# One decoder layer with top-2 experts on one core: routing of the last tiles in fewer, larger batches, in written order

## The chip, the core and the metric

The kernel is one program on one core of a Trainium2 chip. Five engines work side by side, each through its own list of instructions in order: TensorE (PE in the profile, its weight loads PEld), VectorE (DVE), ScalarE (ACT), GpSimd (POOL) and SyncE (SP), which here issues most transfers. The metric is device time of one execution in microseconds (us); less is better.

## What is computed

A layer of a decoder trunk over 1024 tokens (and 16 meta tokens) of width 1024: a mixer of two head groups, an output projection, a layer normalisation, a mixture of experts, a second normalisation. This case is about the seam between the projection and the experts:

```python
mix = mixed @ w_out                                   # output projection
h = layer_norm(ALPHA * h + mix, ln1_g, ln1_b)
group_prob = softmax(h @ w_group + b_group)           # 4 groups: the best one
in_group = (h @ w_expert + b_expert)[best group]      # its 8 experts: the best two
e_w = softmax(top2(in_group))
for e in range(32):                                   # each token: two of 32 experts
    y += combine[:, e] * (silu(h @ w1[e]) * (h @ w3[e])) @ w2[e]
out = layer_norm(ALPHA * h + y, ln2_g, ln2_b)
```

## The kernel before

Tokens lie in eight tiles of 128. The mixer runs first. Its attention of the last two tiles (6 and 7) ends last, so for tiles 0 to 5 the projection, normalisation and logits are woven into the attention (`p3gen`), and for tiles 6 and 7 they follow it.

For a tile t the steps are: `s0(t)` loads the residual `ht` and transposes and splits the mixed heads into two pieces (`mh`, `ml`, since a float32 product is made of three products of pieces); `s1(t)` makes the product (`omm`, two halves of 512 columns, 12 matrix instructions each), adds it to `ht` on VectorE, takes the statistics (`ln_stats`), applies the normalisation (ScalarE, then gain `g` and shift `b` on VectorE) and stores the tile to `h1d` in memory; `s2(t)` transposes `ht` and makes the 36 router logits `lg`. For tiles 6 and 7 the logits are made from the tile as it is before the normalisation.

Routing of tiles t0 to t1 is two functions. `choose(t0, t1)` is a chain of small VectorE instructions: `first_max` finds the first largest logit (twice for the experts), two-hot rows `oh` and their sum `ohs` follow, then the weights `gate` and the table `rv`. `place(t0, t1)` counts on TensorE how many earlier tokens chose the same expert (into `rq`), reads each token's place `pose`, adds to the running count `cum`, and then, for each tile and choice, compares the place with the slot numbers (`ohp`) and multiplies by `rv`, so that the table `acc` tells which token stands in which slot of which expert. When all eight tiles are in `acc`, `index` makes `ix`, and GpSimd gathers the first expert's 128 rows of `h1d` by it.

The experts then run one after another (`phase4`): 128 gathered rows are transposed and split (`xf`, `xh`, `xl`), multiplied by `w13`, gated (`sg`), multiplied by `w2`, and stored to `ysd`. The weights are loaded by SyncE (`load_raw`) into a ring of buffers, long ahead, and each 512-column piece is split into two on ScalarE and VectorE (`split_k`: `w13h` and `w13l`). Of expert 0's eight pieces six are split; two are used as they are. The last two experts' outputs aren't stored, but added in `finish` by a product with a one-hot matrix; the others come back by gathers with the index `fi`.

The order of the steps around the seam is written as a string, which a loop reads:

```python
SEQ3 = "A1 L4 b04 B1 L4 H5 A9 a46 L3 G3 b46 H6 p0 G9 B9 a67 p1 |0 O2 O1 H7 O9 p2 R3 b68 p5"
for w in SEQ3.split():
    steps[w[0]](*[int(x) for x in w[1:]])
```

A and B advance `s0` of tile 6 and 7 by so many steps, G and O advance `s1` of tile 6 and 7, H is `s2`, L loads so many weight blocks of 1 MB, a is `choose` and b is `place` of a range of tiles, p and R also split pieces of expert 0. What stands before the bar is ordered by the framework's scheduler, what stands behind it keeps the written order on every engine. `p3gen` calls `choose` itself for pairs of tiles up to the tile number `CH_`.

Of the kernel before, what the change touches and what calls it, by code (L numbers as in the profile page):

```python
# [8 lines left out]
F32 = mybir.dt.float32  # L9
F32R = mybir.dt.float32r  # L10
I32 = mybir.dt.int32
AF = mybir.ActivationFunctionType
ALU = mybir.AluOpType
AX = mybir.AxisListType.X
# [3 lines left out]
P = 128  # L18
D = 1024
KT = 8  # L20
SEQ = 1024
NT = 8
# [5 lines left out]
NE = 32  # L28
# [8 lines left out]
TV, TO = (0, 1, 2, 3, 4, 5, 6, 7), (0, 0.75, 1.25, 2.5, 3.25, 4, 4.75)  # L37
TA = (0, 1, 2, 3, 4, 5, 6, 7)
SP0 = 0
PX, CH_ = 6, 4  # L40
H0, HG_, GS = 10, (1, 2), (3, 1)
XB2, MH = 2, 2
RX = 1
SPH = (0, 2, 4, 6, 6, 8, 8)
SEQ3 = "A1 L4 b04 B1 L4 H5 A9 a46 L3 G3 b46 H6 p0 G9 B9 a67 p1 |0 O2 O1 H7 O9 p2 R3 b68 p5"
XN = 3
YB = 2
GE = 5
SPK = ()
# [7 lines left out]
G2 = 3  # L57
# [1 line left out]
MB, BB, WB, TB = 2, 2, 2, 3  # L59
RA, RB, RC = 5, 6, 2  # L60
FE, RL = NE - 8, 4 * (RA + RB + 4 + RC) + 4 + RA
RT = 2
GB = 3 * HA * DH
LN_EPS = 1e-5
RMS_EPS = 1e-6
# [16 lines left out]
class Trunk:  # L82
# [738 lines left out]
    def phase2(self):  # L821
        nc, tc, a, r, small = self.nc, self.tc, self.a, self.rows, self.small
# [255 lines left out]
        O, TQ = {}, ["tp", TB, "tg", TG]  # L1078
# [136 lines left out]
            nc.vector.tensor_scalar(rs[:, 1:2], rs[:, 0:1], -1.0, None, op0=ALU.mult)  # L1215
            nc.vector.scalar_tensor_tensor(lg, lg, rs[:, 1:2], cg[:, 1], op0=ALU.mult, op1=ALU.add)

        def choose(t0, t1, hook=lambda i: None):
            n = t1 - t0
            ts = slice(t0, t1)  # L1220
            rp = O["op"]
# [24 lines left out]
            m = first_max(lg[:, :, :4], 4, oh4)  # L1246
            ex = tl("ex", 4)
            nc.vector.tensor_tensor(ex, lg[:, :, :4], bc(m, 4), op=ALU.subtract)
            hook(0)
            sp, sn = tl("sp", 4), tl("sn", 4)  # L1250
            nc.scalar.activation(sp, ex, AF.Sigmoid)
            nc.scalar.activation(sn, ex, AF.Sigmoid, scale=-1.0)
# [10 lines left out]
            m2 = first_max(ing2, 8, oe[1])  # L1263
            e2 = tl("e2")
            nc.vector.tensor_tensor(e2, m1, m2, op=ALU.subtract)
            hook(1)
            for k in range(2):
                nc.scalar.activation(gate[:, ts, k], e2, AF.Sigmoid, scale=1.0 - 2.0 * k)
            for t in range(n):
# [4 lines left out]
            ohs, rv = O["ohs"], O["rv"]  # L1274
# [12 lines left out]
        def place(t0, t1):  # L1287
            n, ts = t1 - t0, slice(t0, t1)
            ohs, rv = O["ohs"], O["rv"]
# [9 lines left out]
            nc.vector.tensor_reduce(pose[:, ts], px, axis=AX, op=ALU.add)  # L1299
            for t in range(t0, t1):  # L1300
                nc.vector.tensor_tensor(cum, cum, ohs[:, t], op=ALU.add)
            pa = ps.tile([P, 4, P], F32, name="rq", bufs=1)[:, 0, :2 * NE]
            for t in range(t0, t1):
                for k in range(2):
# [100 lines left out]
        def run(gen, n=99):  # L1405
            for _ in range(n):
                next(gen, None)
# [2 lines left out]
        o67 = [s1(6), s1(7)]  # L1410
        self.man, self.pcs0 = ExitStack(), {}

        def split(i):
            self.split_k(self.raws_of(0), range(SPH[i], SPH[i + 1]), self.pcs0, SPK)

        steps = {"L": self.load_raw,
                 "A": lambda n: run(n67[0], n), "B": lambda n: run(n67[1], n),
                 "G": lambda n: run(o67[0], n), "O": lambda n: run(o67[1], n), "H": s2, "p": split,
                 "a": choose, "b": place, "R": lambda n: choose(7, 8, lambda i: split(n + i)),
                 "|": lambda n: self.man.enter_context(tc.manual_schedule())}  # L1420
        for w in SEQ3.split():
            steps[w[0]](*[int(x) for x in w[1:]])
        self.index(acc[:, :NE], NE, self.ix)
        nc.vector.tensor_copy(self.gsl, acc[:, NE:])
        pn = ps.tile([P, 4, P], F32, name=TQ[0], bufs=TQ[1])[:, 0]
        nc.tensor.matmul(pn[:, :NE], ones, cum, start=True, stop=True)
        n1 = small.tile([P, NE], I32, name="n1", bufs=1)
# [49 lines left out]
    def phase4(self):  # L1477
# [127 lines left out]
        self.load_raw(RX)  # L1605
        for e in range(XN):
            gat_(e)
        fi = self.small.tile([P, NT, 2], I32, name="fi", bufs=1)
        eo = mp.tile([P, D], F32, name="y", bufs=YB)
        ev = eo[:, :2 * NT * NE].rearrange("p (t k e) -> p t k e", t=NT, k=2)  # L1610
        fv, fo = [eo[:, D - 2 * NT * (i + 1):D - 2 * NT * i].rearrange("p (t k) -> p t k", k=2) for i in range(2)]
        nc.vector.tensor_tensor(ev, self.oh, self.slots[:, None, None, :NE].to_broadcast([P, NT, 2, NE]), op=ALU.mult)
        nc.vector.tensor_reduce(fv, ev, axis=AX, op=ALU.add)
        nc.vector.scalar_tensor_tensor(fv, fv, float(P), self.pose, op0=ALU.mult, op1=ALU.add)
        nc.vector.tensor_scalar(fo, self.pose, float(P), 4096.0, op0=ALU.is_ge, op1=ALU.mult)
        nc.vector.tensor_tensor(fv, fv, fo, op=ALU.add)
        nc.vector.tensor_scalar(fi, fv, float((NE - 2) * P), None, op0=ALU.min)
        xt = xsplit(xpose(XB[0]))
        gat_(XN)
        self.load_raw(2 + RC - RX)  # L1620
        for e in range(NE):
            more = e + 1 < NE
            ph = up(xt, pcs[e])
            if more:
                self.split_k(self.raws_of(e + 1), range(KT), pcs.setdefault(e + 1, {}))
                tps = xpose(XB[(e + 1) % XN])
                gat_(e + 1 + XN)
                sg = swiglu(ph)
                xt = xsplit(tps)
                if e > 0:  # L1630
                    keep(evac(down(act, pcs.pop(e - 1)), self.gsl[:, e - 1:e]), e - 1)
                act = apose(sg)
                self.split_k(self.raws_of(e), range(KT, 12), pcs[e])
            else:
                self.split_k(self.raws_of(e), range(KT, 12), pcs[e], (), True)
                for i in (1, 0):
                    nc.vector.tensor_tensor(oh[i], self.slots[:, None, :].to_broadcast([P, NT, P]),
                                            ixt[:, i, :, None].to_broadcast([P, NT, P]), op=ALU.is_equal)
                sg = swiglu(ph)
                yo = down(act, pcs.pop(e - 1))  # L1640
                act = apose(sg)
                ys = [[mp.tile([P, D], F32R, name=n, bufs=b) for n, b in (("y", YB), ("xg1", 1))]]
                evac2(yo, self.gsl[:, e - 1:e], ys[0])
# [236 lines left out]
```

## Time and profile before

| | |
|---|---|
| median of 3 runs | 1188.87 us (1187.49 to 1192.16) |
| the profiled execution | 1180.65 us, span 1178.9 us |
| busy share of the span | PE 93%, DVE 73%, ACT 54%, POOL 25% |
| mean granted TensorE clock | 0.957 of full speed |
| mean DMA rate | 230 GB/s |

The span runs from the first to the last instruction of the program; the 1.75 us that the profiled execution takes beyond it lie around the program. A row of the trace gives the start, the duration, the engine, the line, the output and the inputs; a bracket behind it gives how long the engine had been idle and what ended that. Attention ends at about 750 us, the experts run from about 808 to 1124 us, and the last stage from there to the end.

### The profile page before, as it was taken

Reading aid. Unit: us, or ns where it says so; the run is one execution under the profiler, and the core shown is the slowest. Engines: PE = TensorE matmul, PEld = TensorE weight load, DVE = VectorE, ACT = ScalarE, POOL = GpSimd, SP = SyncE. Lnnn points to the kernel's source line nnn. Section 1 sums busy time; section 2 is a strip of 40 time slices with the busy share of each in tenths; the row PEclk is TensorE's granted clock in tenths of the full one; section 3 lists DMA queues with packets and bytes.
Section 4 is the critical chain, followed back from the end, with each engine's and each line's share of the span. In section 5 each row is a group of like instructions: output and inputs, shape, how many; then the busy total and the mean of one; then the engine's idle time right before and its main releaser. Section 6 shows DMA issues by size and latency. Waiting matters only on the chain. (4 is left out here: it accounts for less than half of the span.)

```text
span 1178.9 us, 19811 instructions
## 1 busy us (share of the span) xinstructions
PE 1091.0 (93%) x7061; PEld 932.1 (79%) x7061; DVE 862.4 (73%) x1672; ACT 630.9 (54%) x1310; POOL 289.6 (25%) x389
## 2 busy tenths in 40 slices
PE   6999999999989979899989999866999999999983
PEld 5999999999979968777777777755777777777751
DVE  7941357988532337999848768786999999999946
ACT  3443345755223334556546445234777777777643
POOL 3523102511100013435414322001111111112163
PEclk8999999999989998999989999886999999999997
DMA  7511123457696577886567582576999999599785
GB/s 288 182 59 46 42 93 127 135 166 237 210 241 203 167 246 237 243 231 201 156 199 178 134 297 73 236 281 219 377 398 398 398 406 399 204 366 416 291 213 206
DMA packets 112441, 271.01 MB, mean 230 GB/s; under 512 B 31075, under 2 KB 60523, under 8 KB 99540
## 3 DMA queue, kind: packets, MB, share of 16 engines
q1 hardware_dynamic: 100816, 236.43, 58.4%
q0 software_dynamic: 11232, 32.22, 8.4%
q8 instruction: 57, 0.93, 0.3%
q10 hardware_dynamic: 292, 1.07, 0.2%
q14 instruction: 44, 0.36, 0.1%
HBM read 213.83 MB, written 64.53 MB: 236 GB/s over the span
## 5 line engine op out<-in xcount | busy, mean ns | idle before, releaser
L186 PE MATMUL pj<-hTh,wfh 128*128 128x346 f32 (+1 forms) x480 | 156.3, 326 | 0.0
L187 PE MATMUL pj<-hTl,wfh 128*128 128x346 f32 (+1 forms) x480 | 156.0, 325 | 0.0
L188 PE MATMUL pj<-hTh,wfl 128*128 128x346 f32 (+1 forms) x480 | 155.9, 325 | 0.0
L881 DVE TENSOR_TENSOR_SCAN mm<-mm,zero 128x272 f32<-128x272 f32 (+3 forms) x64 | 89.4, 1410 | 22.0 <-ACT mm L868 19.8
L186 PEld LDWEIGHTS pj<-hTh,wfh 128*128 128x128 f32 x480 | 91.0, 190 | 0.4 <-issue 0.2
L188 PEld LDWEIGHTS pj<-hTh,wfl 128*128 128x128 f32 x480 | 91.0, 190 | 0.1
L187 PEld LDWEIGHTS pj<-hTl,wfh 128*128 128x128 f32 x480 | 90.9, 189 | 0.2
L1535 PE MATMUL ph<-w13h,xh 128*128 128x512 f32 x192 | 88.8, 463 | 0.0
L179 PE MATMUL pj<-wvh,hTl 128*128 128x256 f32 (+3 forms) x280 | 79.7, 287 | 2.6 <-DVE hTl L97 2.6
L178 PE MATMUL pj<-wvl,hTh 128*128 128x256 f32 (+3 forms) x280 | 79.7, 287 | 2.1 <-DVE wvl L97 2.1
L177 PE MATMUL pj<-wvh,hTh 128*128 128x256 f32 (+3 forms) x280 | 80.2, 290 | 0.0
L1465 DVE TENSOR_TENSOR w13l<-raw,w13h 128x512 fp32r<-128x512 f32 x126 | 77.8, 683 | 0.0
L1503 POOL DMA_INDIRECT xg<-h1d,ix x32 | 34.1, 1067 | 171.3 <-PE tp L1513 134.1
L1537 PE MATMUL ph<-w13h,xl 128*128 128x512 f32 x192 | 75.4, 393 | 0.0
L1536 PE MATMUL ph<-w13l,xh 128*128 128x512 f32 x192 | 74.9, 390 | 0.0
L872 POOL TENSOR_SCALAR_AFFINE_SELECT mm<-mm 128x128 f32<-128x128 f32 x64 | 40.2, 634 | 113.5 <-ACT mm L868 113.3
L1464 ACT ACTIVATE w13h<-raw 128x512 fp32r<-128x512 f32 x126 | 68.0, 620 | 0.0
L866 PE MATMUL z<-qk 128*128 128x416 f32 (+6 forms) x224 | 60.7, 378 | 5.8 <-ACT kuw L778 3.8
L868 ACT ACTIVATE mm<-z 128x512 f32<-128x512 f32 (+1 forms) x80 | 44.3, 564 | 40.7 <-PE z L866 31.0
L1465 DVE TENSOR_TENSOR w2l<-raw,w2h 128x512 fp32r<-128x512 f32 x96 | 59.9, 687 | 2.2 <-ACT w2h L1464 0.2
L96 ACT ACTIVATE xh<-tp 128x512 fp32r<-128x512 f32 x64 | 31.5, 492 | 49.9 <-DVE xf L1522 43.1
L902 ACT ACTIVATE wt<-tp 128x512 f32<-128x512 f32 (+1 forms) x80 | 41.6, 556 | 27.2 <-PE tp L901 26.6
(441 smaller groups left out, 2965.8 us busy)
## 6 DMA issues: line engine op xcount, KB each, us to landing
raw<-in_w SPq DMA_DIRECT2D x67, 1024.0 KB, 11.1
ysd<-y POOLq DMA_DIRECT2D x30, 512.0 KB, 8.4
qk<-qkd SPq DMA_DIRECT2D x16, 520.0 KB, 5.8
ht<-hscr SPq DMA_DIRECT2D x16, 512.0 KB, 3.4
wo4h<-in_w SPq DMA_DIRECT2D x8, 1024.0 KB, 12.4
wo4l<-in_w SPq DMA_DIRECT2D x7, 1024.0 KB, 13.3
wo6l<-in_w SPq DMA_DIRECT2D x7, 1024.0 KB, 11.9
wo6h<-in_w SPq DMA_DIRECT2D x7, 1024.0 KB, 10.6
```

The source lines that it names most:

```text
L177: nc.tensor.matmul(o[:p, :n], xh, wh[:, kt, ws], start=(kt == 0), stop=False)
L178: nc.tensor.matmul(o[:p, :n], xh, wl[:, kt, ws], start=False, stop=False)
L179: nc.tensor.matmul(o[:p, :n], xl, wh[:, kt, ws], start=False, stop=(kt == KT - 1))
L186: nc.tensor.matmul(o[:, :n], wh[:, kt], self.hTh[:, kt, c0:c0 + n], start=(kt == 0), stop=False)
L187: nc.tensor.matmul(o[:, :n], wh[:, kt], self.hTl[:, kt, c0:c0 + n], start=False, stop=False)
L188: nc.tensor.matmul(o[:, :n], wl[:, kt], self.hTh[:, kt, c0:c0 + n], start=False, stop=(kt == KT - 1))
L881: nc.vector.tensor_tensor_scan(mm[:, c0:c1][:, ::-1], mm[:, c0:c1][:, ::-1], self.zero1.to_broadcast([P, c1 - c0]), 1.0, op0=ALU.mult, op1 ...
L1464: nc.scalar.activation(wh, raw, AF.Copy)
L1465: (nc.gpsimd if k in pool else nc.vector).tensor_tensor(wl, raw, wh.bitcast(F32), op=ALU.subtract)
L1535: nc.tensor.matmul(ph, xh[:, kt], wh, start=False, stop=False)
L1536: nc.tensor.matmul(ph, xh[:, kt], wl, start=False, stop=False)
L1537: nc.tensor.matmul(ph, xl[:, kt], wh, start=False, stop=(kt == ks[-1]))
```

## The change

- `choose` is called for tiles 0 and 1, 2 to 5, and 6 and 7 (three calls; before: 0 and 1, 2 and 3, 4 and 5, 6, 7). `place` is cut in two: `place` (count, `pose`, `cum`) and `fill` (`ohp`, `acc`), each called for tiles 0 to 5 and then for 6 and 7 (before: 0 to 3, 4 and 5, 6 and 7).
- The bar stands near the front of the string, so that nearly all of the seam keeps the written order.
- All six splits of expert 0 are made in one piece, behind `index`.
- The last three weight blocks of the string are loaded behind the work on tile 7.
- The six instructions that make `fi` move from behind the first gathers to the last expert, ahead of its `w2` splits.

```diff
-PX, CH_ = 6, 4
+PX, CH_ = 6, 2
-SPH = (0, 2, 4, 6, 6, 8, 8)
-SEQ3 = "A1 L4 b04 B1 L4 H5 A9 a46 L3 G3 b46 H6 p0 G9 B9 a67 p1 |0 O2 O1 H7 O9 p2 R3 b68 p5"
+SEQ3 = "A1 B1 L4 L4 |0 H5 A9 B9 a26 G2 x06 O1 G1 y06 O1 H6 O1 G9 H7 O9 L3 a68 x68 y68"
-RT = 2
+RT = 4
-        def choose(t0, t1, hook=lambda i: None):
+        def choose(t0, t1):
...
             for t in range(t0, t1):
                 nc.vector.tensor_tensor(cum, cum, ohs[:, t], op=ALU.add)
+
+        def fill(t0, t1):
+            rv = O["rv"]
             pa = ps.tile([P, 4, P], F32, name="rq", bufs=1)[:, 0, :2 * NE]
             for t in range(t0, t1):
...
-        def split(i):
-            self.split_k(self.raws_of(0), range(SPH[i], SPH[i + 1]), self.pcs0, SPK)
-
-                 "G": lambda n: run(o67[0], n), "O": lambda n: run(o67[1], n), "H": s2, "p": split,
-                 "a": choose, "b": place, "R": lambda n: choose(7, 8, lambda i: split(n + i)),
+                 "G": lambda n: run(o67[0], n), "O": lambda n: run(o67[1], n), "H": s2,
+                 "a": choose, "x": place, "y": fill,
...
         self.index(acc[:, :NE], NE, self.ix)
         nc.vector.tensor_copy(self.gsl, acc[:, NE:])
+        self.split_k(self.raws_of(0), range(KT), self.pcs0)
...
         for e in range(XN):
             gat_(e)
-        fi = self.small.tile([P, NT, 2], I32, name="fi", bufs=1)
-        eo = mp.tile([P, D], F32, name="y", bufs=YB)
...
-        nc.vector.tensor_scalar(fi, fv, float((NE - 2) * P), None, op0=ALU.min)
         xt = xsplit(xpose(XB[0]))
...
             else:
+                fi = self.small.tile([P, NT, 2], I32, name="fi", bufs=1)
+                eo = mp.tile([P, D], F32, name="y", bufs=YB)
...
+                nc.vector.tensor_scalar(fi, fv, float((NE - 2) * P), None, op0=ALU.min)
                 self.split_k(self.raws_of(e), range(KT, 12), pcs[e], (), True)
```

What this does to the order of the instructions is seen at three places. The first is VectorE behind the choice of tile 5's batch: `rv` closes a choice, `px` and `pose` read the counts of `place`, `ohp` are the one-hot rows that TensorE waits for. Before (the batch of tiles 4 and 5, placed in a batch of its own):

```order
L1285 TENSOR_TENSOR rv<-oh,val 128x4x32
L1285 TENSOR_TENSOR rv<-oh,gate 128x4x32
L1142 SCALAR_TENSOR_TENSOR ht<-ht,o 128x512
L108 BN_STATS lnst<-ht 128x6
L1142 SCALAR_TENSOR_TENSOR ht<-ht,o 128x512
L1298 TENSOR_TENSOR px<-oh,rq 128x128
L1301 TENSOR_TENSOR cum<-cum,ohs 128x32
L108 BN_STATS lnst<-ht 128x6
L1299 TENSOR_REDUCE pose<-px 128x4
L1301 TENSOR_TENSOR cum<-cum,ohs 128x32
L110 BN_AGGR lnmv<-lnst 128x2
L1306 TENSOR_SCALAR ohp<-slots,pose 128x128 x3
```

The same place in the change (the batch of tiles 2 to 5, then the placing of tiles 0 to 5):

```order
L1282 TENSOR_TENSOR rv<-oh,val 128x8x32
L1282 TENSOR_TENSOR rv<-oh,gate 128x8x32
L1141 SCALAR_TENSOR_TENSOR ht<-ht,o 128x512 x2
L1295 TENSOR_TENSOR px<-oh,rq 128x384
L1296 TENSOR_REDUCE pose<-px 128x12
L1298 TENSOR_TENSOR cum<-cum,ohs 128x32 x6
L1141 SCALAR_TENSOR_TENSOR ht<-ht,o 128x512
L107 BN_STATS lnst<-ht 128x6 x2
L109 BN_AGGR lnmv<-lnst 128x2
L100 TENSOR_SCALAR lnrs<-lnmv 128x1
L1306 TENSOR_SCALAR ohp<-slots,pose 128x128 x12
```

The work of two placings (tiles 0 to 3, and 4 and 5) has moved into one, twelve one-hot rows stand in a piece, and three additions to `ht` and tile 6's statistics stand ahead of them.

The second place is VectorE from the last normalisation to the choice of the last batch. Before (tile 7; tile 6 was chosen earlier, under the products of tile 7):

```order
L1188 SCALAR_TENSOR_TENSOR lnrs<-lnmv,lnrs 128x1
L1192 TENSOR_TENSOR ht<-ht,g_6699 128x512 x2
L1192 TENSOR_TENSOR ht<-ht,b_6700 128x512 x2
L1465 TENSOR_TENSOR w13l<-wo4l,w13h 128x512 x2
L1231 TENSOR_REDUCE fm<-lg 128x1
L1234 SCALAR_TENSOR_TENSOR fu<-lg,fm,desc 128x4
```

The same place in the change (tiles 6 and 7):

```order
L107 BN_STATS lnst<-ht 128x6 x2
L109 BN_AGGR lnmv<-lnst 128x2
L100 TENSOR_SCALAR lnrs<-lnmv 128x1
L1187 SCALAR_TENSOR_TENSOR lnrs<-lnmv,lnrs 128x1
L1191 TENSOR_TENSOR ht<-ht,g_6699 128x512 x2
L1191 TENSOR_TENSOR ht<-ht,b_6700 128x512 x2
L1213 SCALAR_TENSOR_TENSOR lg<-cg,lnmv,tq 128x36
L1214 TENSOR_SCALAR lnrs<-lnrs 128x1
L1215 SCALAR_TENSOR_TENSOR lg<-lg,lnrs,cg 128x36
L1187 SCALAR_TENSOR_TENSOR lnrs<-lnmv,lnrs 128x1
L1191 TENSOR_TENSOR ht<-ht,g_6699 128x512 x2
L1191 TENSOR_TENSOR ht<-ht,b_6700 128x512 x2
```

The normalisations of both tiles now stand one behind the other, ahead of the choice, and two splits of expert 0 have gone from there.

The third place is SyncE, which issues transfers in order. Before (`raw` is a weight block of 1 MB, `h1d` the stored tiles 5, 6 and 7):

```order
L1194 DMA h1d<-ht 128x1024
L1119 DMA ht<-hscr 128x1024
L1452 DMA raw<-in_w 128x2048 x11
L1194 DMA h1d<-ht 128x1024 x3
L1452 DMA raw<-in_w 128x2048 x2
L1452 DMA wo4h<-in_w 128x2048
```

The same place in the change:

```order
L1450 DMA raw<-in_w 128x2048
L1118 DMA ht<-hscr 128x1024
L1450 DMA raw<-in_w 128x2048 x7
L1193 DMA h1d<-ht 128x1024 x3
L1450 DMA raw<-in_w 128x2048 x5
L1450 DMA wo4h<-in_w 128x2048
```

Three blocks have moved behind the store of tile 7, and one stands ahead of a load of `ht`.

## Rows read from the trace of the kernel before

**Rows 1.** One stretch of the experts: length, busy us of PE, PEld, DVE, ACT, POOL; clock; DMA share; GB/s.

```profile
900.00:1000.00 100.00, 100.00 (x457) 76.70 (x456) 95.87 (x177) 78.77 (x157) 16.44 (x20) 1.00 1.00 397
```

**Rows 2.** Waits from 740 to 820: engine, tile, what ended them; us, times, longest.

```profile
PE rq L1291 <- DVE ohs L1275: 12.8, 2, 9.5
```

**Rows 3.** Timeline: tile 5, its last product and the end of its normalisation.

```profile
749.74 0.40 PE L1141 MATMUL tg<-w13h,ml 128*128 128x512 f32 x1
...
756.75 1.22 DVE L1184 TENSOR_TENSOR ht<-ht,b 128x1024 f32<-128x1024 f32 x1
```

**Rows 4.** Timeline: the choice of tiles 4 and 5 on VectorE, first and last row.

```profile
764.28 0.16 DVE L1231 TENSOR_REDUCE fm<-lg 128x2 f32<-128x8 f32 x1
...
769.12 0.28 DVE L1285 TENSOR_TENSOR rv<-oh,gate 128x128 f32<-128x128 f32 x1
```

**Rows 5.** VectorE from 751 to 802 by form: count, busy us, mean ns.

```profile
L108 DVE BATCH_NORM_STATS2 lnst<-ht 128x6 f32<-128x512 f32 x5 | 3.4, 685 | 0.0
...
L1142 DVE SCALAR_TENSOR_TENSOR ht<-ht,o 128x512 f32<-128x512 f32 x4 | 2.7, 676 | 0.0
...
L1301 DVE TENSOR_TENSOR cum<-cum,ohs 128x32 f32<-128x32 f32 x8 | 1.5, 184 | 0.0
...
L1298 DVE TENSOR_TENSOR px<-oh,rq 128x256 f32<-128x256 f32 x1 | 0.4, 422 | 1.0 <-PE rq L1296 1.0
```

**Rows 6.** Stretches of 2 us behind a wait of PE, columns as in rows 1.

```profile
756.00:758.00 2.00, 1.39 (x7) 1.39 (x7) 2.00 (x6) 0.00 (x0) 0.00 (x0) 0.50 0.95 393
...
760.00:762.00 2.00, 2.00 (x17) 1.95 (x16) 1.34 (x9) 1.19 (x2) 0.00 (x0) 0.81 1.00 418
```

**Rows 7.** Timeline: four one-hot rows times the table, at either clock.

```profile
774.27 1.08 PE L1307 MATMUL rq<-rv,ohp 128*128 128x64 f32 x8
...
799.35 1.94 PE L1307 MATMUL rq<-rv,ohp 128*128 128x64 f32 x8 [1.31 <-DVE ohp L1306]
```

**Rows 8.** Timeline: from the last product of tile 7 to the index.

```profile
780.50 0.39 PE L1141 MATMUL o<-w13h,ml 128*128 128x512 f32 x1
...
787.88 1.24 ACT L120 ACTIVATE ht<-ht,lnrs 128x1024 f32<-128x1024 f32 x1 [1.81 <-issue]
...
790.36 1.29 DVE L1192 TENSOR_TENSOR ht<-ht,b 128x512 f32<-128x512 f32 x2
...
791.56 1.29 DVE L1465 TENSOR_TENSOR w13l<-wo4l,w13h 128x512 fp32r<-128x512 f32 x2
...
792.76 0.15 DVE L1231 TENSOR_REDUCE fm<-lg 128x1 f32<-128x4 f32 x1
...
797.61 0.22 DVE L1285 TENSOR_TENSOR rv<-oh,gate 128x64 f32<-128x64 f32 x1
798.07 0.29 DVE L1298 TENSOR_TENSOR px<-oh,rq 128x128 f32<-128x128 f32 x1 [0.24 <-PE rq L1296]
...
801.79 0.19 DVE L1475 SCALAR_TENSOR_TENSOR ix<-acc,ie 128x32 int32<-128x32 f32 x1
```

**Rows 9.** Timeline of SyncE: two weight blocks issued behind the store of tile 7.

```profile
792.12 2.08 SPq L1452 DMA_DIRECT2D raw<-in_w  x2
```

**Rows 10.** Gathers: median us from issue to landing, 800 to 812, then 900 to 1000.

```profile
xg<-h1d,ix POOLq DMA_INDIRECT x4, 4.6
...
xg<-h1d,ix POOLq DMA_INDIRECT x10, 8.4
```

**Rows 11.** Timeline: the index of the combine, first and last of six rows.

```profile
803.18 0.69 DVE L1612 TENSOR_TENSOR y<-oh,slots 128x512 f32<-128x512 f32 x1
...
805.13 0.43 DVE L1617 TENSOR_SCALAR fi<-y 128x16 int32<-128x16 f32 x1
```

**Rows 12.** Timeline: the last expert on VectorE, and what TensorE waits for.

```profile
1113.99 2.49 DVE L1465 TENSOR_TENSOR w13l<-wo4h,w13h 128x512 fp32r<-128x512 f32 x4
...
1119.69 0.41 PE L1550 MATMUL ta<-ident,sg 128*128 128x128 f32 x2 [0.70 <-DVE sg L1544]
...
1126.50 0.77 PE L1782 MATMUL pf<-y,xg 128*128 128x512 f32 x1 [2.88 <-DVEq L1693]
```

More of the change, by code (lines that the diff above doesn't have):

```diff
@@ L1248, in choose @@
             nc.vector.tensor_tensor(ex, lg[:, :, :4], bc(m, 4), op=ALU.subtract)
-            hook(0)
             sp, sn = tl("sp", 4), tl("sn", 4)
@@ L1265, in choose @@
             nc.vector.tensor_tensor(e2, m1, m2, op=ALU.subtract)
-            hook(1)
             for k in range(2):
@@ L1607, in phase4 @@
             gat_(e)
-        fi = self.small.tile([P, NT, 2], I32, name="fi", bufs=1)
-        eo = mp.tile([P, D], F32, name="y", bufs=YB)
[L1610 to L1616, printed above, removed]
-        nc.vector.tensor_scalar(fi, fv, float((NE - 2) * P), None, op0=ALU.min)
         xt = xsplit(xpose(XB[0]))
@@ L1634, in phase4 @@
             else:
+                fi = self.small.tile([P, NT, 2], I32, name="fi", bufs=1)
+                eo = mp.tile([P, D], F32, name="y", bufs=YB)
+                ev = eo[:, :2 * NT * NE].rearrange("p (t k e) -> p t k e", t=NT, k=2)
+                fv, fo = [eo[:, D - 2 * NT * (i + 1):D - 2 * NT * i].rearrange("p (t k) -> p t k", k=2) for i in range(2)]
+                nc.vector.tensor_tensor(ev, self.oh, self.slots[:, None, None, :NE].to_broadcast([P, NT, 2, NE]), op=ALU.mult)
+                nc.vector.tensor_reduce(fv, ev, axis=AX, op=ALU.add)
+                nc.vector.scalar_tensor_tensor(fv, fv, float(P), self.pose, op0=ALU.mult, op1=ALU.add)
+                nc.vector.tensor_scalar(fo, self.pose, float(P), 4096.0, op0=ALU.is_ge, op1=ALU.mult)
+                nc.vector.tensor_tensor(fv, fv, fo, op=ALU.add)
+                nc.vector.tensor_scalar(fi, fv, float((NE - 2) * P), None, op0=ALU.min)
                 self.split_k(self.raws_of(e), range(KT, 12), pcs[e], (), True)
```

## The prediction

> **What bounds the kernel now.** I read the stretches by stage first. While the experts run, TensorE is busy in every microsecond at full clock, 457 instructions in 100 us, 0.22 us each, and VectorE stands at 96% [rows 1]. Nothing in that part has room to take up a late start, so whatever delays the first expert delays the end by as much. Then I read the waits of the seam, where TensorE isn't the bound: it waits twice for `ohs`, 12.8 us in all, once for 9.5 [rows 2]. The seam ends when the index is formed at 801.98 us (start 801.79 and 0.19), and the chain up to there is read in order of time: last product of tile 7, normalisation, choice, placing, index [rows 8]. The question is when this chain ends in the changed order, and what else moves.
>
> **The sum goes against the profiled execution**, 1180.65 us (span 1178.9). The timed runs of the same kernel have a median of 1188.87, so I add the same microseconds to that. A half per cent, about what a measurement of this kernel can tell from no change, is 5.9 us.
>
> **Term 1, up to the last product of tile 7.** Taking the choice of tiles 2 and 3 out of the time of tile 5's normalisation is a gain. Between tile 5's last product (749.74) and the end of its shift row (756.75 and 1.22, so 757.97) VectorE runs some two dozen small choice instructions [rows 3]; the steps of the chain itself come to about 7.0 us, so tile 5 is ready at some 756.8, 1.2 us earlier. The choice of tiles 4 and 5 began at 764.28 [rows 4]; the new one, with all else ahead of it alike, begins at about 763.1.
>
> That choice took 5.1 us for two tiles (764.28 to 769.12 and 0.28) [rows 4]. For four tiles in written order I add 0.6 for six more small rows of the two tiles, 0.3 for wider rows, and 1.3 for the seven rows that make the weights, which before filled gaps between dependent rows and now stand one behind the other: a choice in written order is 27 steps from 792.76 to 797.61, 0.18 us each [rows 8]. Together 7.3, so it ends at 770.4. Ahead of the first one-hot row VectorE then has three additions to `ht` (0.68 each), two statistics (0.69 each), six additions to `cum` (0.18 each), `px` and `pose` of six tiles (0.42 for four, so 0.55 each), and 0.35 of small rows [rows 5]: 5.9 us, so the first `ohp` stands at about 776.3. TensorE is done sooner: 24 products at 0.22 from about 762, a short wait for `ohs`, the counts, 12 products of tile 7: about 773. It waits some 3.3 us, where before it was busy.
>
> A wait of that length costs the clock. In the trace TensorE stood still from 753.3 to 756.6, then worked at 0.50, the lower level of 1.2 GHz, and was back in part (0.81) in the stretch from 760 [rows 6]. Four one-hot rows times the table take 1.94 us at the lower clock and 1.08 at the higher [rows 7]. Twelve of them, eight at the lower: 4.9 us (3.2 at full clock). They end at 781.3, the twelve products left at 784.1. Before, the last product ended at 780.89 [rows 8]. **Term 1 is +3.2**; if the clock stays up +1.6, if tile 5 isn't earlier +4.4.
>
> **Term 2, from there to the index.** Before, 21.1 us [rows 8]. In the new order the logits of tile 6, the statistics of tile 7 and the normalisation of tile 6 come behind the last product. Before, ScalarE began tile 7's normalisation 7.0 us behind it (780.89 to 787.88); VectorE gave about 1.8 of these to splits and to tile 6's choice, which are gone, so tile 6's normalisation begins after 5.2 us. A normalisation from ScalarE's start to the last shift row took 3.8 us (787.88 to 791.65). Two of them now stand in series, since ScalarE copies tile 7's transposed rows only behind its work on tile 6, and the logits of tile 7 (0.9) lie between: 8.5 us. The choice up to `px` took 5.3 for one tile (792.76 to 798.07); for two I add 1.0 (three rows more of comparing, three of the second tile, wider rows). From `px` to the index 3.9 as before. 5.2 + 8.5 + 6.3 + 3.9 = 23.9. The two splits that stood ahead of the choice (1.29 us [rows 8]) are counted as gone in it. **Term 2 is +2.8**; if the choice of two runs as the one of rows 4 did, +1.6. The index is formed at about 808.
>
> **Costed at nothing.** The six splits behind the index are 3.9 us of VectorE at 0.65 each (1.29 for two [rows 8]), the counts of overflow behind them 1.4. They lie under the first gather, 4.6 us from issue to landing [rows 10], with its issue ahead and transposes behind it; without that cover they would cost 3.9. Three weight blocks go behind the store of tile 7; they belong to experts 3 to 5, and a block is 2.6 us at the 397 GB/s of rows 1.
>
> **Term 3, the gather.** These blocks aren't free for the queue. Before, two blocks were issued at 792.12 behind the store of tile 7 [rows 9], and gathers landed in 4.6 us; in the loaded stretch from 900 they took 8.4 [rows 10]. Now five blocks and the store start at about 798, 5.5 MB, 14 us, up to about 812, when the first gather is under way from 809. Most of the queue has been worked off by then, so I take +1.0 between 0 and 3.8, nearer the quiet row. The Trainium skill, DMA: Bandwidth & Descriptors, section Queues, rings and completion order, says that each DMA engine takes packets from its queues in turn; by that the gather would share with the blocks rather than stand behind them, which also leaves it between the two ends.
>
> **Term 4, the last expert.** The six rows of `fi` took 2.4 us (803.18 to 805.56) [rows 11], under the first gather, where VectorE had nothing to do. They now stand ahead of the last splits, begun at 1113.99, and VectorE has no gap from there to `sg`, for which TensorE waits already 0.70 at 1119.69; the last stage starts at 1126.50, when VectorE comes to the branch [rows 12]. So 2.4 are paid in full, TensorE's wait grows to 3 us, and its clock falls for half of the twelve products behind it, +1.0 (up to 2.5 if all). **Term 4 is +3.4**, from 2.4 to 4.9.
>
> Sum: 3.2 + 2.8 + 1.0 + 3.4 = **+10.4 us**, 1191.1 for a profiled execution and 1199.3 for the median. With all lower ends 1.6 + 1.6 + 0 + 2.4 = +5.6, with all upper ends 4.4 + 2.8 + 3.8 + 4.9 = +15.9.
>
> **Rivals.** *The low ends*: the clock holds through waits of 3 us and the gather doesn't feel the blocks. For it: the fall is read behind one wait here. Against it: that wait was 3.3 us, as long as these [rows 6]. It gives +5.6, 1194.5, within half a per cent; chance 0.15.
>
> *Fewer batches pay*, the case on the other side. A small row costs nearly the same for one tile or two (0.15 and 0.16, first rows of the choices in rows 8 and 4), so two calls of `choose` fewer save 2 x 5.1 us of VectorE less 2 x 1.5 for wider calls, 7.2 us, and the 3.3 us wait of TensorE for the first placing is gone. If all 7.2 lay on the path, less term 4, the end would come 3.8 us earlier, 1185.1. It decides if the last choice begins before 791 (I have it at 797.8). Against it: the saved rows lay under TensorE's products before, and the row before the last choice is a normalisation, not VectorE's load. Chance 0.06. The Trainium skill, Perfetto Trace Analysis, section Optimizing Scalar/DVE Operations, gives such an overhead per instruction (about 60 ns) and recommends grouping if the engine is saturated; the rows agree on the overhead. The same section says that breaking work up may end it sooner where an engine only causes bubbles, which fits this seam better.
>
> *The gather takes the loaded time and the clock is low throughout*: +15.9, 1204.8, chance 0.15. For it: the blocks are in flight when it is issued.
>
> **The numbers.** Forecast +10.4 holds 0.64. The range reaches from the low ends less 3 us, since the saved rows may give some back, to the upper ends: 1191 to 1205. Faster by over half a per cent 0.04 (part of the second rival); within 0.17; slower 0.79.
>
> **What would show it.** Right, if `px` of six tiles comes at about 772, the first one-hot row at 776, the last product of tile 7 ends at 784 with a lower clock ahead of it, the two normalisations follow in series, the index stands at 808, TensorE waits some 3 us for `sg` in the last expert, and the experts take as long as before. Wrong, if TensorE finds the one-hot rows ready, if the index stands before 804, or if the experts' stretch gets shorter.

## The result, and the profile after

The changed kernel takes 1201.94 us (median of 3 runs, 1198.82 to 1206.3) against 1188.87; the ratio is 1.0135 with a 95% interval from 1.009 to 1.0181. The change costs 13.1 us where 10.4 were forecast. Its profiled execution is the median one: 1201.94 us, span 1200.2, mean granted clock 0.947. The profile shown of before is 8 us below its own median, so the two profiles lie 21.3 us apart; where these 8 us come from is asked in run 1 below.

The experts run as before: TensorE busy throughout, full clock, one stretch of 100 us of the changed kernel (columns as in [rows 1]):

```profile
900.00:1000.00 100.00, 100.00 (x461) 76.78 (x460) 95.83 (x177) 78.60 (x157) 16.41 (x20) 1.00 1.01 400
```

TensorE's waits from 740 to 830 (engine, tile, what ended them; us, times, longest), which answer to [rows 2]. Of the two waits for `ohs` before, the one of 3.3 us is gone and the long one is left. The waits for the gather and for the one-hot rows have grown; those for tile 5 and for the copies of tile 7's transposed rows are new. Two rows of before, and then the change:

```profile
PE tp L1513 <- DMA xg<-h1d,ix: 5.8, 1, 5.8
PE rq L1307 <- DVE ohp L1306: 1.3, 1, 1.3
```

```profile
PE tp L1511 <- DMA xg<-h1d,ix: 9.9, 1, 9.9
PE rq L1288 <- DVE ohs L1272: 9.2, 1, 9.2
PE rq L1307 <- DVE ohp L1306: 4.4, 2, 3.1
PE tq L1202 <- DVE ht L1183: 3.6, 1, 3.6
PE tq L1207 <- ACT h1T L1203: 3.6, 2, 3.3
```

The chain of the seam in order of time (timeline of the changed kernel; answers to [rows 3, 4, 8]). The first row, which closes the statistics of tile 4, is the zero of the table below:

```profile
742.70 0.16 DVE L114 SCALAR_TENSOR_TENSOR lnrs<-lnmv,lnrs 128x1 f32<-128x1 f32 x1 [0.72 <-POOL lnrs L101]
...
759.22 1.12 PE L1202 MATMUL tq<-ident,ht 128*128 128x128 f32 x4 [3.64 <-DVE ht L1183]
...
767.74 0.16 DVE L1230 TENSOR_REDUCE fm<-lg 128x4 f32<-128x16 f32 x1
...
776.36 0.55 DVE L1295 TENSOR_TENSOR px<-oh,rq 128x384 f32<-128x384 f32 x1
...
781.30 4.04 PE L1307 MATMUL rq<-rv,ohp 128*128 128x64 f32 x24 [3.08 <-DVE ohp L1306]
...
789.77 0.39 PE L1140 MATMUL o<-w13h,ml 128*128 128x512 f32 x1
...
795.75 1.24 ACT L119 ACTIVATE ht<-ht,lnrs 128x1024 f32<-128x1024 f32 x1 [3.96 <-issue]
...
797.52 3.63 PE L1207 MATMUL tq<-wg,h1T 128*128 128x36 f32 x16 [3.29 <-ACT h1T L1203]
...
802.07 1.24 ACT L119 ACTIVATE ht<-ht,lnrs 128x1024 f32<-128x1024 f32 x1 [4.12 <-issue]
...
806.32 3.26 SPq L1450 DMA_DIRECT2D raw<-in_w  x5
...
815.69 0.19 DVE L1473 SCALAR_TENSOR_TENSOR ix<-acc,ie 128x32 int32<-128x32 f32 x1
...
825.47 1.97 PE L1511 MATMUL tp<-ident,xg 128*128 128x128 f32 x8 [9.91 <-DMA xg<-h1d,ix]
```

Read from the top: TensorE stands still 3.64 us for tile 5, and 3.08 us for the twelve one-hot rows; behind the last product two normalisations follow in series (ScalarE's part at 795.75 and at 802.07), with tile 7's logits between them; five weight blocks are issued 9.6 us ahead of the end of the index row; the gather is waited for 9.91 us. The last expert (answers to [rows 12]):

```profile
1139.89 0.41 PE L1548 MATMUL ta<-ident,sg 128*128 128x128 f32 x2 [2.63 <-DVE sg L1542]
...
1147.61 0.47 PE L1780 MATMUL pf<-y,xg 128*128 128x512 f32 x1 [2.22 <-DVEq L1691]
```

### The profile page after: what moved, and what is told of

Read it like the earlier page. It is cut to its first block, busy times and chain, and to the rows that moved or that the text cites. A ratio compares the mean times of both kernels' runs of the same rounds, so it can differ in the third digit from the quotient of the medians.

```text
span 1200.2 us, 19743 instructions
## 1 busy us (share of the span) xinstructions
PE 1099.9 (92%) x7059; PEld 939.5 (78%) x7059; DVE 859.6 (72%) x1619; ACT 629.7 (52%) x1302; POOL 285.7 (24%) x389
## 5 line engine op out<-in xcount | busy, mean ns | idle before, releaser
L176 PE MATMUL pj<-wvh,hTh 128*128 128x256 f32 (+3 forms) x280 | 79.6, 288 | 0.2 <-ACT hTh L95 0.2
L871 POOL TENSOR_SCALAR_AFFINE_SELECT mm<-mm 128x128 f32<-128x128 f32 x64 | 36.5, 577 | 116.3 <-ACT mm L867 115.9
L871 POOL TENSOR_SCALAR_AFFINE_SELECT be<-be 128x128 f32<-128x128 f32 x64 | 43.2, 684 | 54.1 <-ACT be L868 45.0
```

What stands on the lines that cost most here:

```text
L176: nc.tensor.matmul(o[:p, :n], xh, wh[:, kt, ws], start=(kt == 0), stop=False)
L871: nc.gpsimd.affine_select(out=v[:, e - P:e], in_=v[:, e - P:e], pattern=[[-1, P]], compare_op=ALU.is_gt, fill=fill, base=0, channel_multip ...
```

## The experiments

Twelve runs followed, each timed against the kernel before on the same chip; the chip is not the same in all of them, so ratios compare with the kernel before and not with one another. The columns are those of one profiled execution each. The times in this table are us behind the zero row of each profile (740.42 in the profile shown of before), so what happens ahead of the seam drops out. The columns: the choice of the batch with tile 5 begins; the last product of tile 7 ends; the index row ends; the first transposes of gathered rows begin; the last stage begins.

| kernel | choice | last product | index | transposes | last stage | ratio, 95% interval |
|---|---|---|---|---|---|---|
| before, profile shown ahead | 23.9 | 40.5 | 61.6 | 67.1 | 386.1 | |
| 1 before again | 26.7 | 44.9 | 65.8 | 71.5 | 389.6 | 0.998, 0.9962 to 0.9999 |
| the change | 25.0 | 47.5 | 73.2 | 82.8 | 404.9 | 1.0135, 1.009 to 1.0181 |
| 2 change, `fi` back | 25.0 | 47.5 | 73.2 | 82.9 | 401.9 | 1.0085, 1.0064 to 1.0107 |
| 3 change, blocks in front | 25.0 | 47.5 | 73.2 | 79.6 | 401.5 | 1.0095, 1.0061 to 1.013 |
| 4 change, idle products | 23.9 | 46.4 | 70.3 | 80.0 | 401.1 | 1.0061, 1.0039 to 1.0083 |
| 5 before, `fi` late | 26.7 | 44.8 | 65.7 | 71.4 | 393.4 | 1.0038, 1.0013 to 1.0063 |
| 6 before, splits behind | 26.7 | 45.0 | 62.0 | 68.3 | 386.5 | 0.997, 0.9948 to 0.9991 |
| 7 change, order alone | 25.0 | 47.5 | 73.2 | 79.3 | 398.0 | 1.0068, 1.005 to 1.0087 |
| 8 as 7, tile 6 early | 25.0 | 41.6 | 67.9 | 74.0 | 392.4 | 1.0021, 1.0002 to 1.004 |
| 9 as 8, choice over normalisation | 25.0 | 41.5 | 64.8 | 74.5 | 392.3 | 1.0058, 1.0036 to 1.008 |
| 10 as 6, choice over normalisation | 23.7 | 40.4 | 55.9 | 64.7 | 382.9 | 0.9977, 0.9947 to 1.0007 |
| 11 as 10, idle products | 23.8 | 40.4 | 59.6 | 70.0 | 385.7 | 1.0017, 0.999 to 1.0045 |
| 12 as 9, idle products | 25.1 | 41.6 | 70.5 | 80.0 | 395.3 | 1.005, 1.0027 to 1.0074 |

Run 1 is the kernel before itself, and came out at 0.998: ratios closer to one than about 0.3% say nothing, and the columns must tell.

**Run 1, the kernel before once more**, no edit.

> The kernel before, unchanged, for a second profile. The first one (1180.65 us) lies 7 us below the lowest timed run, so 8 of the 21.3 us between the two profiles can't be the change. Theory: the seam from tile 5 to the index (757.97 to 801.98 in the first profile) is repeatable within 1.5 us and the 8 us lie in other stages, mostly where TensorE's granted clock is below full (attention, 400 to 740 us). Rival: the seam of the first profile was itself a lucky one, with a higher clock, and an ordinary one is 5 us longer or more. Ratio 1.000, within 0.4% either way.

Median 1188.05 us; the profile is the median execution (span 1186.3). Its seam is not the one shown ahead: the last product comes 4.4 us later. Two stretches of 6 us behind TensorE's restart, first of the profile shown ahead, then of this run (columns as in [rows 1]):

```profile
756.60:762.60 6.00, 5.99 (x37) 5.95 (x38) 3.91 (x16) 1.23 (x3) 0.00 (x0) 0.65 1.02 425
762.60:768.60 6.00, 6.00 (x37) 5.28 (x37) 5.45 (x37) 1.17 (x5) 0.00 (x0) 1.00 1.00 423
```

```profile
759.50:765.50 6.00, 6.00 (x30) 5.96 (x31) 3.57 (x13) 1.20 (x2) 0.00 (x0) 0.50 1.01 426
765.50:771.50 6.00, 6.00 (x26) 5.70 (x26) 3.27 (x18) 0.90 (x3) 0.00 (x0) 0.50 1.01 425
```

The program and the wait ahead are the same; the granted clock came back to full some 4 us behind the restart in the one, some 13 in the other. Among the profiles of the old seam (before, runs 1, 5, 6, 10, 11) the choice begins at 23.7 to 23.9 in three and at 26.7 in three. So the profile that carried the prediction was a lucky one at this place, against my own theory that the seam repeats within 1.5 us. The 7.4 us between the spans of the two profiles are 2.6 ahead of the zero row, 3.5 from there to the last stage, and 1.3 in that stage. From here on the change is read against run 1.

**Run 2, the rows of `fi` back behind the gathers.** The rest as in the change.

```diff
+        fi = self.small.tile([P, NT, 2], I32, name="fi", bufs=1)
...
         xt = xsplit(xpose(XB[0]))
...
-                fi = self.small.tile([P, NT, 2], I32, name="fi", bufs=1)
```

> The changed kernel with the six rows of fi back behind the first gathers. Theory (term 4): 3.1 us less than the changed kernel, about 1199 and a ratio to before of 1.011; in the profile TensorE's wait for sg in the last expert goes from 2.63 back to about 0.7 us, and the twelve products behind it take 3 us again instead of 4. Rival: the last expert hides them, ratio as for the changed kernel (1.0135).

The wait for `sg` fell from 2.63 to 0.61 us, and from the first gathered transposes to the last stage it took 319.0 us in place of 322.1: -3.1, as expected.

**Run 3, the three blocks in front.**

```diff
-SEQ3 = "A1 B1 L4 L4 |0 H5 A9 B9 a26 G2 x06 O1 G1 y06 O1 H6 O1 G9 H7 O9 L3 a68 x68 y68"
+SEQ3 = "A1 B1 L4 L4 L3 |0 H5 A9 B9 a26 G2 x06 O1 G1 y06 O1 H6 O1 G9 H7 O9 a68 x68 y68"
```

> The changed kernel with the three weight blocks issued with the other eight, ahead of the stores of tiles 5 to 7. Theory (term 3, sized too small in the forecast): the first gather no longer shares the engines with them; from the index to the first transposes of the gathered rows about 5.5 us as in the kernel before, against 9.6 in the changed one; 4 us less than the changed kernel, about 1198, ratio 1.010. Rival: the gather is late because it follows the store of tile 7 closely, or because of the blocks of the ring that stay there; then still 8 us or more.

From the index to the transposes it took 6.4 us in place of 9.6, and the last stage began 3.4 us earlier. The ratio alone doesn't show it: the timed runs spread from 1192.75 to 1207.31 us, and the interval overlaps that of the change. The transfers around the first gather, of the change and of this run (columns as in [rows 1], the last two the DMA share and GB/s):

```profile
816.00:824.00 8.00, 0.00 (x0) 0.00 (x0) 4.60 (x12) 1.22 (x2) 3.75 (x3) 0.50 1.00 418
824.00:826.00 2.00, 0.53 (x3) 0.54 (x4) 0.00 (x0) 0.00 (x0) 0.00 (x0) 0.50 0.51 197
```

```profile
820.00:824.00 4.00, 0.20 (x1) 0.07 (x1) 3.93 (x10) 1.87 (x2) 2.27 (x2) 0.50 0.07 7
824.00:827.00 3.00, 0.12 (x1) 0.12 (x2) 1.29 (x7) 0.00 (x0) 1.49 (x2) 0.50 0.88 303
```

In the change the engines are full until 824, in this run they stand still when the index is ready. The blocks in flight are worth 3.2 us, not the 1.0 of term 3.

**Run 4, products of the identity with itself where TensorE waits**: 9 ahead of tile 5's transposes, 8 ahead of the first placing's products, 8 behind the transposes of tile 7, 18 behind its logits, 24 under the gather. Nothing reads their results.

```diff
+        def warm(n):
+            d = ps.tile([P, 4, P], F32, name="rq", bufs=1)[:, 0]
+            for _ in range(n):
+                nc.tensor.matmul(d, self.ident, self.ident, start=True, stop=True)
...
-SEQ3 = "A1 B1 L4 L4 |0 H5 A9 B9 a26 G2 x06 O1 G1 y06 O1 H6 O1 G9 H7 O9 L3 a68 x68 y68"
+SEQ3 = "A1 B1 L4 L4 |0 w9 H5 A9 B9 a26 G2 x06 O1 w8 G1 y06 O1 H6 O1 G9 H7 O9 L3 w9 w9 a68 x68 y68"
```

> The changed kernel with products of the identity by itself, whose results are thrown away, in five waits of TensorE: 9 ahead of tile 5's transposes, 8 ahead of the one-hot rows of tiles 0 to 5, 8 between transposes and logits of tile 7, 18 ahead of the last placing, 24 behind it. Theory (the miss of terms 1 and 2 is the clock): the granted clock stays at full in the seam; 2 us less up to the choice, 2 less in the products of tile 7, 1.5 less in its logits, 1.5 less in the last placing, 2 to 3 less in expert 0; 7 to 9 us less than the changed kernel, about 1194, ratio 1.005. Rival: VectorE's chain sets the time and the clock costs nothing: ratio 1.0135 or, as the extra products stand in TensorE's way, more.

The last product came 1.1 us earlier and the index 2.9, the last stage 3.8. From the last product to the index it took 23.9 us in place of 25.7, so 1.8 us of this stretch went with the clock, net of the products' own time: the 16 products of tile 7's logits took 1.98 us there in place of 3.63 in the change. The 7 to 9 us weren't reached: the clock still fell to 0.50 in part of the waits.

**Run 5, `fi` late in the kernel before**: the diff of run 2 the other way round.

> The kernel before with one part of the change alone: the six rows of fi moved into the last expert. Theory (term 4): TensorE's wait for sg grows from 0.70 to about 2.6 us and the stretch from there to the last stage by 0.9 us, +3.1 us together, ratio 1.0026. Rival: the six rows find a place in the last expert when the seam in front of it is the old one, no wait beyond 0.7, ratio 1.000. Beside it the trace gives a third reading of the old seam: from the last statistics of tile 4's normalisation to the last product of tile 7 the two profiles of the kernel before read 40.5 and 44.9 us; I expect one of the two, by how fast the clock comes back behind the restart.

TensorE's wait for `sg` is 2.64 us again, and from the transposes to the last stage it took 322.02 us against 318.07 in run 1: +3.95, of which 1.94 up to the end of the wait and 2.01 behind it. The part costs alone about what it costs in the change (3.1 in run 2).

**Run 6, all splits of expert 0 behind the index in the kernel before.**

```diff
-SEQ3 = "A1 L4 b04 B1 L4 H5 A9 a46 L3 G3 b46 H6 p0 G9 B9 a67 p1 |0 O2 O1 H7 O9 p2 R3 b68 p5"
+SEQ3 = "A1 L4 b04 B1 L4 H5 A9 a46 L3 G3 b46 H6 G9 B9 a67 |0 O2 O1 H7 O9 a78 b68"
...
         nc.vector.tensor_copy(self.gsl, acc[:, NE:])
+        self.split_k(self.raws_of(0), range(KT), self.pcs0, SPK)
```

> The kernel before with one part of the change alone: all six splits of expert 0 stand behind the index, and the choice of tile 7 has no splits in it. Theory: the two splits that stood ahead of the last choice are gone from the chain (1.3 us earlier index), the six behind the index lie under the first gather (5.5 to 5.7 us from the index to the first gathered transposes, no longer than before): -1.3 us, ratio 0.999. Rival: they aren't hidden, VectorE comes late to the copies of the gathered rows, and 2 to 4 us are added behind the first transposes: ratio 1.001 to 1.003.

The index comes 3.7 us earlier, more than expected, the transposes 3.2, the last stage 3.1. The splits were in the way twice: ScalarE's normalisation of tile 7 begins 4.1 us behind the last product in place of 6.8, and the choice begins sooner behind it. Rows of this run, of run 1 behind it:

```profile
785.34 0.40 PE L1141 MATMUL o<-w13h,ml 128*128 128x512 f32 x1
...
789.88 1.24 ACT L120 ACTIVATE ht<-ht,lnrs 128x1024 f32<-128x1024 f32 x1 [0.84 <-POOL lnrs L102]
...
802.60 0.19 DVE L1476 SCALAR_TENSOR_TENSOR ix<-acc,ie 128x32 int32<-128x32 f32 x1
```

```profile
787.55 0.40 PE L1141 MATMUL o<-w13h,ml 128*128 128x512 f32 x1
...
794.70 1.24 ACT L120 ACTIVATE ht<-ht,lnrs 128x1024 f32<-128x1024 f32 x1 [1.59 <-issue]
...
808.62 0.19 DVE L1475 SCALAR_TENSOR_TENSOR ix<-acc,ie 128x32 int32<-128x32 f32 x1
```

It is the quickest median of all runs (1182.96 us, 1187.89 before on the same chip) and, of the parts that ran alone, the one that pays. Its ratio, 0.997, lies close to what run 1 gave with nothing changed; the columns carry this reading.

**Run 7, order and batches alone**: the edits of runs 2 and 3 together.

> The changed kernel with the rows of fi back behind the gathers and the three weight blocks in front: what is left is the order and the batches of choice and placing, and the splits behind the index. Theory: the two parts add up, -3.1 (fi) and -3.2 (blocks), so some 6.5 to 7.5 us above the kernel before, ratio 1.006; index 73.2 us behind the statistics of tile 4's normalisation as in the change, 6.4 from there to the first gathered transposes, wait for sg 0.6. Rival: the parts overlap (what is won at the gather is lost again behind it), ratio 1.009 or more.

The two parts add up within 0.6 us: the last stage 6.9 us ahead of the change (3.0 and 3.4 apart), ratio 1.0068. What is left of the change, order and batches with the splits behind the index, costs 8.4 us against run 1, and 11.5 against run 6, which has the splits in the same place.

**Run 8, tile 6 early**: logits and normalisation of tile 6 ahead of the second half of tile 7's product.

```diff
-SEQ3 = "A1 B1 L4 L4 L3 |0 H5 A9 B9 a26 G2 x06 O1 G1 y06 O1 H6 O1 G9 H7 O9 a68 x68 y68"
+SEQ3 = "A1 B1 L4 L4 L3 |0 H5 A9 B9 a26 G2 x06 O1 G1 H6 G9 O1 y06 O1 H7 O9 a68 x68 y68"
```

> As the run with the order alone, with one further move: logits and normalisation of tile 6 stand ahead of the second half of tile 7's product and of the one-hot rows of tiles 0 to 5, so that only one normalisation is left behind the last product. Theory: the index came late because two normalisations stand in series behind the last product (10.1 us from the first one's start to the last shift row); with one of them moved the index comes 4 to 6 us earlier, ratio 1.001 to 1.003, with the same few batches. Rival: the fewer, wider batches themselves cost the time, or what is moved is paid in front as TensorE then waits longer for the one-hot rows: the index stays within 1.5 us, ratio 1.005 or more.

The index came 5.3 us earlier and the last stage 5.6, with the same three calls of `choose`. Rows of this run:

```profile
781.45 0.39 PE L1140 MATMUL o<-w13h,ml 128*128 128x512 f32 x1
784.74 3.48 PE L1307 MATMUL rq<-rv,ohp 128*128 128x64 f32 x24 [2.90 <-DVE ohp L1306]
...
789.82 3.63 PE L1207 MATMUL tq<-wg,h1T 128*128 128x36 f32 x16
...
794.36 1.24 ACT L119 ACTIVATE ht<-ht,lnrs 128x1024 f32<-128x1024 f32 x1 [3.81 <-DVE lnrs L1187]
...
807.99 0.19 DVE L1473 SCALAR_TENSOR_TENSOR ix<-acc,ie 128x32 int32<-128x32 f32 x1
```

The gain doesn't lie behind the last product, as the expectation had it: from there to the index it took 26.3 us (25.7 in run 7), since the one-hot rows and their products now stand there in place of the first normalisation. It lies in front: the last product came 5.9 us earlier, with tile 6's normalisation under it. So more than half of the 8.4 us was the two normalisations in series and the place of the one-hot rows, which this edit moves together; some 1 us of it is the clock's, as the second half of tile 7's product ran at full clock (3.0 us, 4.0 in run 7). The run is still 5.9 us behind run 6 at the last stage.

**Run 9, the choice over ScalarE's part of the normalisation.** The step `O` is cut once more behind `ln_apply` of tile 7, and the choice put between.

```diff
                 self.ln_apply(ht, P, rs, ht)
+                if t == 7:
+                    yield
...
-SEQ3 = "A1 B1 L4 L4 L3 |0 H5 A9 B9 a26 G2 x06 O1 G1 H6 G9 O1 y06 O1 H7 O9 a68 x68 y68"
+SEQ3 = "A1 B1 L4 L4 L3 |0 H5 A9 B9 a26 G2 x06 O1 G1 H6 G9 O1 y06 O1 H7 O1 a68 O9 x68 y68"
```

> The run with tile 6 early, and the choice of tiles 6 and 7 put between ScalarE's part of tile 7's normalisation and VectorE's part of it. Theory: VectorE no longer stands still while ScalarE works (1.4 us) and TensorE's counts lie under the gain and shift rows, so the index comes 1.4 to 2.5 us earlier than there (67.9 us behind the statistics of tile 4), ratio 1.000 to 1.001. Rival: VectorE's rows add up to the same, index within 0.5 us, ratio 1.002.

**Run 10, the same cut in run 6** (`H7 O1 a78 O9 b68` in place of `H7 O9 a78 b68`).

> The kernel before with all splits behind the index, and the choice of tile 7 put between ScalarE's part of its normalisation and VectorE's. Theory: as in the run above, the index comes 1.4 us or more ahead of 62.0 us, ratio 0.9955 to 0.996. Rival: nothing to be had, 0.997 as with the splits alone.

In run 9 the index is 3.1 us earlier than in run 8, and the transposes 0.5 later. In run 10, counted from the last product, the index is 1.5 us earlier than in run 6 (15.5 against 17.0) and the transposes 1.1 later. What was won at the index was lost at the gather, by the mechanism of run 3: the store of tile 7, with two blocks behind it on the queue, is now issued 3.8 us ahead of the end of the index (run 8: 10.0). Timeline of run 9, and then the transfers behind the index, of run 9 and of run 8:

```profile
801.67 1.21 SPq L1452 DMA_DIRECT2D raw<-in_w  x2
...
804.83 0.19 DVE L1475 SCALAR_TENSOR_TENSOR ix<-acc,ie 128x32 int32<-128x32 f32 x1
```

```profile
803.00:811.00 8.00, 1.69 (x9) 1.55 (x8) 6.37 (x18) 2.00 (x2) 3.20 (x3) 0.50 1.01 364
808.00:812.00 4.00, 0.00 (x0) 0.00 (x0) 3.98 (x9) 1.52 (x2) 2.62 (x2) 0.50 0.11 14
```

My theory saw the index and not the queue behind the store, the same slip as in the prediction. The ratio of run 9 is 0.4% above that of run 8, while the profiles agree within 0.1 us at the last stage. They ran on different chips, and each profile is of the fastest execution of its run (1185.62 and 1185.85 us); that difference stays open.

**Run 11, idle products in run 10**: 45 behind tile 7's logits, 36 behind the last table rows (`w9 w9 w9 w9 w9` ahead of `a78`, and `warm(36)` behind the count).

> As the run before this one, with 81 products of the identity with itself, whose result nothing reads: 45 behind the logits of tile 7, 36 behind the last table rows, while the first gather is under way (each 0.12 us at full clock). Theory: the low clock behind tile 7's logits costs the one-hot products, the transposes and the first products of the first expert some 3 to 4 us (TensorE is back at full clock only 5 to 6 us behind the first gathered transposes); with TensorE busy the clock stays up: ratio 0.992 to 0.993. Rival: the clock falls in spite of them or they stand in front of the counts, no gain: 0.996 or more.

**Run 12, idle products in run 9**, at three places: 27 ahead of tile 5's transposes, 45 and 36 as in run 11.

> The few batches of the change, with tile 6 early and the choice over ScalarE's part of the normalisation, and such products of the identity at three places: 27 in the wait for tile 5's normalisation, 45 behind the logits of tile 7, 36 under the first gather. Theory: the written order lets them stand where TensorE waits, the clock holds through the restart too (the choice of tiles 2 to 5 comes 3 us earlier, at about 23 us behind the statistics of tile 4), and 3 us more behind the last product: ratio 0.995. Rival: a clock that falls in spite of them, ratio 1.000, and so few batches are no gain whatever stands around them.

Both theories fell on a price. The 45 products leave 90 records, two for each product, so in run 11 they take 11.6 us in place of the 5.4 I had counted, and stand in front of the counts; the 36 leave 72 and take 10.8, and the transposes of the gathered rows begin right behind them, with no wait for the gather left. Run 11:

```profile
787.29 11.59 PE L1421 MATMUL rq<-ident 128*128 128x128 f32 x90
798.93 0.43 PE L1293 MATMUL rq<-ohs,triS 128*128 128x64 f32 x2
...
803.05 10.81 PE L1421 MATMUL rq<-ident 128*128 128x128 f32 x72
813.91 1.09 PE L1523 MATMUL tp<-ident,xg 128*128 128x128 f32 x8
```

The index comes 3.7 us later than in run 10 (run 12: 5.7 later than in run 9), the transposes 5.3 (5.5). That the clock is worth something shows behind the gather: from the transposes to the last stage run 11 took 315.7 us in place of 318.1, run 12 315.3 in place of 317.8, and the first eight transposes took 1.09 us in place of 1.94 and 1.97. In run 12 the clock held through the restart, and the choice of tiles 2 to 5 came no earlier (25.1), since the 27 products, 6.7 us up to the next work, kept tile 5's transposes waiting until 762.14, 19.5 behind the zero row (16.5 in the change). With nine there, run 4 had the choice at 23.9 (25.0 in the change), though its clock still fell; a number between, and fewer products at the other two places, were not tried.

## Why the prediction came out as it did

**Sum.** +10.4 us was forecast, 1191 to 1205; 1201.94 (+13.1) lies inside. Between run 1 and the change, both median executions, the last stage begins 15.4 us later: 2.6 up to the last product, 4.9 to the index, 3.9 to the transposes, 4.1 to the last stage (each rounded). That is 5.0 more than forecast and close to the sum of the upper ends (+15.9). The last stage was 1.1 us shorter in the change's profile and its zero row 0.4 earlier, which leaves 13.9 between the spans; that the medians came nearer to the forecast than the seam did is luck. Of the signs named ahead, the lower clock, the two normalisations in series and the wait for `sg` came. The times did not: counted from the zero row, the first one-hot row came 2.3 us later than forecast, the last product 3.8 and the index 5.6.

**Term 1** was +3.2; against run 1 it is +2.6, and so near by chance. Tile 5's choice begins 1.7 us earlier (1.2 forecast), and from it to the first one-hot row it took 13.1 us, as worked out (13.2). TensorE waits 3.08 us for the one-hot rows (3.3). Their products take 4.04 (4.9), as the clock fell only some 1.4 us behind their start. The products of tile 7 left behind them took 5.1 us, from 785.1 to 790.2, where I counted 2.8, since I had the clock back by then. The base had moved as well: run 1's own last product is 4.4 us later than that of the profile I worked from, and against that profile the term reads +7.0, outside its bounds. What failed there is the use of one execution's recovery of the clock [rows 6] as if it were the kernel's.

**Term 2** was +2.8 and is +4.9, over its upper end. The step "Two of them now stand in series" was right, and its "8.5 us" is what was mis-sized: they took 10.1 us, from 795.75 to 805.83. The other steps came as worked out, 5.6 us up to the first normalisation (5.2), 6.2 for the choice up to `px` (6.3), 3.9 from there to the index (3.9). Tile 7's logits between the two normalisations were costed at 0.9 us; they began 3.29 us behind TensorE's last work, as they waited for ScalarE, and took 3.63 at a granted clock of 0.50. Run 4 gives 1.8 us of the term to the clock, and run 8 shows that the index comes 5.3 us earlier when tile 6 has its place ahead of the last product and the one-hot rows behind it.

**Term 3** was +1.0 and is +3.9, at its upper end (3.8). The failed step is "most of the queue has been worked off by then": the blocks were to be through 3 us behind the start of the gather; they were issued at 806.32, the first gather at 816.78, and the transfers were full until 824, 7 us behind that, with a further load of 1 MB, `wo4h`, issued at 818.40, that the 5.5 MB left out. Gathers from 812 to 826 landed in 8.4 us, the loaded figure of [rows 10], in place of 4.5 in run 1. With the three blocks in front 3.2 of the 3.9 us are gone (run 3). The Trainium skill, DMA: Bandwidth & Descriptors, section Queues, rings and completion order, lets each engine take packets from its queues in turn; the gathers did get through beside the loads, with 11 to 15% of the engines' time from 819 to 824, but their landing took as long as in the loaded stretch, so the rule told me that it isn't stuck, and not that it is cheap.

**Term 4** was +3.4 and is +3.1 by run 2, +4.0 by run 5, +4.1 between run 1 and the change. The wait for `sg` of 3 us came as 2.63, and the stretch behind it took 7.7 us in place of 6.8.

**Costed at nothing**, the six splits behind the index: right. In run 6 they add 0.5 us between index and transposes (6.2 against 5.7), and taking them out of the seam gives 3.7 us at the index; the prediction had 3.1 of this in term 2 (1.8 and 1.3).

**The rivals.** *The gather takes the loaded time and the clock is low throughout* was nearest to what happened: the gathers took 8.4 us, the clock stood at 0.50 from some 6 us behind the last product to beyond the first gathered transposes, and the 15.4 us of the columns lie by its +15.9. I had given it 0.15. *The low ends* are out: the clock did not hold, and the gather felt the blocks. *Fewer batches pay* is out for this change. What the number of batches costs or saves by itself stays open: run 8, with tile 6 in a better place, and the blocks and `fi` of before, is 5.9 us behind run 6 at the last stage, but the two differ in written against scheduled order and in the place of the one-hot rows too, which no run took apart. The Trainium skill, Perfetto Trace Analysis, section Optimizing Scalar/DVE Operations, says that breaking work up can end it sooner where an engine only causes bubbles; these two runs fit that and don't show it.

## What to carry to other kernels

Where a program ends a stage with a chain that nothing covers, count what stands in series in it, and look first for what can lie under the last big product (here tile 6's normalisation, run 8), before counting instructions saved. An index that comes earlier can be worth nothing if a bulk transfer is issued shortly ahead of the gather that uses it (runs 9 and 10): price the queue from the moment of its issue to its last byte. And take a second profile of the kernel before, since a clock that falls and comes back can make one execution 4 us better at the place under study.

## What the runs showed that I had not expected

- The same wait of TensorE, in kernels that are alike up to there, was followed by 3 to 4 us or by some 13 us at the lower clock (0.50, 1.2 GHz), in three profiles each, with TensorE at work all the time; in the changed order, behind a wait of 3.6 us, it was 9 to 10 us in all six profiles without idle products. In two of the quick ones (before, run 11) the clock had fallen to 0.50 already 13 to 14 us behind the zero row, some 2.5 us earlier than in runs 1, 5 and 6; in the third (run 10) it fell as late as in those and was back as early all the same. Why is open.
- The zero row itself lies between 740.22 and 747.33 us in profiles of kernels that are alike up to there, so the mixer ahead varies by up to 7 us between executions; the granted clock between 400 and 500 us was 0.90 in run 1 and 0.86 in run 3.
- A float32 product of the 128 by 128 identity with itself leaves two records, one 0.11 us behind the other at full clock: 27 of them stood 6.7 us in front of the next work in run 12, some 0.25 a product and not 0.12.
